# Row loads and stores of a DoRA forward kernel on one DMA ring in a fixed order

## The chip, the cores and the metric

The kernel runs on one core of one Trainium2 chip. The time is device microseconds (us) of one execution. A profile shows one execution under the hardware profiler; its span (163.3 us for the kernel before) is about 1.8 us shorter than the device time.

## The reference

```python
x: (16, 2048, 256) f32     W: (256, 256)     lora_A: (256, 16)     lora_B: (16, 256)     m: (256,)
W_adapted = W + scale * (lora_A @ lora_B)
W_final = W_adapted / sqrt(sum(W_adapted ** 2, axis=0) + 1e-8) * m
y = x.reshape(-1, 256) @ W_final           # (32768, 256) f32, as large as x
```

`W_final` is small. The work is to read 33.55 MB of `x`, multiply each row by a 256 x 256 matrix, and write 33.55 MB of `y`.

## The kernel before

The rows go through in 8 blocks of 4096 rows, 4.19 MB each. A block is loaded into one of five buffers by SyncE. TensorE transposes it in 8 chunks, VectorE copies a chunk to bf16, TensorE multiplies, and ScalarE copies the product back over the same place of the block's buffer. When the block is done, ScalarE issues its store. So there are two rings of DMA work: SyncE's with all loads and ScalarE's with all stores.

```python
xpool = ctx.enter_context(tc.tile_pool(name="xpool", bufs=5))
def load_x(b):
    t = xpool.tile([P, DJ, IN], FP32, name="x_sb", tag="x_sb")      # 128 x 32 x 256: 32 KB a partition
    nc.sync.dma_start(out=t, in_=x_flat[b * BLK : (b + 1) * BLK].rearrange("(p j) k -> p j k", p=P))
    return t
# ... loads of W, lora_A, lora_B, m; w_final is computed in about 17 us ...
for b in range(NBLK):                      # 8
    x_sb = load_x(b)
    for c in range(DJ // J):               # 8 chunks
        # ... 8 transposes into xt_ps, cast to xt_sb (VectorE), 8 matmuls into y_ps ...
        nc.scalar.copy(out=x_sb[:, c * J : (c + 1) * J, :], in_=y_ps)
        if c + 1 in store_after[b]:        # at the block's end; the last block in three parts
            nc.scalar.dma_start(out=..., in_=x_sb[:, j0:j_stored, :])
```

Below, L0 to L7 are the loads of the blocks and S0 to S7 their stores.

## Time and profile before

| what | value |
|---|---|
| time | 165.1 us, median of 3 runs (165.06 to 165.16) |
| span of the profile | 163.3 us |
| DMA rings | loads 48.9%, stores 48.0% of the 16 engines' span |
| rate while only loads run (5 to 35 us) | 428 to 432 GB/s |
| rate while both rings run (50 to 125 us) | 428 to 433 GB/s |
| rate while only stores run (130 to 155 us) | 429 to 432 GB/s |
| a 32 KB packet, median, on either ring | 1213 ns |
| first transposes, last copy of a result | 14 us, 151.3 us |

The rates are the bytes of the trace's DMA packets in stretches of 5 us, a packet's bytes spread over its time. Here are lines of the page of the kernel before: the span, the rows of 40 equal time slices (each digit is a busy share in tenths, 9 meaning 90% or more, and the last row is GB/s), the two rings with packets, megabytes and share of 16 engines' time, and the shares of the chain of work that ended last.

```profile
span 163.3 us, 2370 instructions
...
PE   0049888888888888888888888898889888886000
...
DMA  6999998999999899999999999999999999999992
GB/s 197 414 474 401 449 450 381 474 425 377 389 425 474 385 470 425 387 482 409 421 466 393 458 429 393 492 393 421 474 401 441 429 409 466 409 413 429 407 425 86
...
q1 hardware_dynamic: 1424, 33.82, 48.9%
q10 hardware_dynamic: 1746, 33.59, 48.0%
...
PE 57%; DVE 26%; DMA 4%; issue 2%; ACT 1%; DVEq 1%; ACTq 1%
```

The reader is to see two things that seem to contradict each other. The DMA row is at 9 (twice 8) from the second slice to the last but one: the 16 DMA engines never rest. Yet the chain that ended last is 57% TensorE and 26% VectorE, as if compute were the limit. The end of that chain, in order of time (start, length, what), settles it:

```profile
149.20 1.06 PE y_ps L158 x8
...
150.28 1.01 ACT x_sb L165
```

The last result is copied at 150.3 us and its store is issued at 151.3 us, but the span is 163.3 us long and the last store lands at 162.3 us. A store of 1 MB alone is an estimated 2.4 us of work at 431 GB/s; it took 11 us because other stores were ahead of it. So two things run side by side: a chain of compute of some 137 us, hidden, and a stream of transfers that starts at 2 us, never stops and ends at 162 us. The stream looks like the limit; e1 and e2 below test it. Its rate is 428 to 433 GB/s in the table above.

SyncE's own waits in the kernel before (in total, times, longest) show that the later loads wait for a buffer to be stored, which is harmless while the engines have other work:

```profile
SPq L52 <- DMA out_dram<-x_sb: 92.8, 3, 54.9
```

### The profile page before, as it was taken

What the parts mean: (1) busy time and instruction counts of PE and PEld (TensorE: products, weight loads), DVE (VectorE), ACT (ScalarE), POOL (GpSimd) and SP (SyncE); (2) the same over time, 40 slices, a digit from 0 to 9 for tenths busy, and PEclk for the clock granted to TensorE, in tenths of its full rate; (3) what the DMA queues carried; (4) which work ended last, traced back from release to release, by engine and by line L of the source; (5) the groups of instructions that cost most, each with busy time, mean ns of one, the idle gap of its engine ahead of it and who ended that gap; (6) DMA issues with size and microseconds to landing.
All of it is one profiled execution on the core that took longest, in us unless ns stands there. A gap on an engine that the chain in (4) does not pass through costs nothing.

```text
span 163.3 us, 2370 instructions
## 1 busy us (share of the span) xinstructions
PE 125.4 (77%) x1034; PEld 107.9 (66%) x1034; DVE 81.1 (50%) x76; ACT 66.1 (40%) x67; POOL 0.7 (0%) x6
## 2 busy tenths in 40 slices
PE   0049888888888888888888888898889888886000
PEld 0028677777777777777778777777887777774000
DVE  0145755555555555554555455545554555455000
ACT  3001244443544444444444364427441844085000
POOL 1000000000000000000000000000000000000000
PEclk9999999999999999999999999999999999999955
DMA  6999998999999899999999999999999999999992
GB/s 197 414 474 401 449 450 381 474 425 377 389 425 474 385 470 425 387 482 409 421 466 393 458 429 393 492 393 421 474 401 441 429 409 466 409 413 429 407 425 86
DMA packets 3180, 67.55 MB, mean 414 GB/s; under 512 B 593, under 2 KB 866, under 8 KB 866
## 3 DMA queue, kind: packets, MB, share of 16 engines
q1 hardware_dynamic: 1424, 33.82, 48.9%
q10 hardware_dynamic: 1746, 33.59, 48.0%
q8 instruction: 8, 0.13, 0.3%
q14 instruction: 2, 0.02, 0.0%
HBM read 33.85 MB, written 33.55 MB: 413 GB/s over the span
## 4 chain that ended last, share of the span: by engine, by line
PE 57%; DVE 26%; DMA 4%; issue 2%; ACT 1%; DVEq 1%; ACTq 1%
PE y_ps L158 33%; DVE xt_sb L153 23%; PE xt_ps L147 22%; DMA m_row<-in_m_dram 4%; PE n_ps L115 1%; DVE rnorm L124 1%; DVEq L206 1%; PE mb_ps L91 1%; ACT x_sb L165 1%; DVE w_final L126 0%; DVE sq L110 0%; DVE wa L106 0%; ACTq L60 0%; ACTq L64 0%; ACT norm L119 0%
## 5 line engine op out<-in xcount | busy, mean ns | idle before, releaser
L153 DVE CAST xt_sb<-xt_ps 128x1024 bf16<-128x1024 f32 x64 | 75.4, 1220 | 56.6 <-PE xt_ps L147 42.2
L165 ACT COPY x_sb<-y_ps 128x1024 f32<-128x1024 f32 x64 | 64.1, 1013 | 72.5 <-PE y_ps L158 72.4
L158 PE MATMUL y_ps<-w_final,xt_sb 128*128 128x256 bf16 x512 | 65.5, 273 | 11.5 <-DVE xt_sb L153 11.5
L147 PE MATMUL xt_ps<-identity,x_sb 128*128 128x128 f32 x512 | 68.7, 279 | 3.4 <-DVE xt_sb L153 3.1
L147 PEld LDWEIGHTS xt_ps<-identity,x_sb 128*128 128x128 f32 x512 | 58.7, 144 | 7.8 <-DVE xt_sb L153 6.7
L158 PEld LDWEIGHTS <-xt_sb 128*128 128x128 bf16 x512 | 47.8, 98 | 22.8 <-DVE xt_sb L153 18.2
L91 PE MATMUL mb_ps<-m_row,ones 1*128 1x256 f32 x2 | 1.2, 694 | 4.6 <-DMA m_row<-in_m_dram 4.6
L119 ACT ACTIVATE norm<-n_ps,eps_col 128x256 f32<-128x256 f32 x1 | 0.5, 473 | 10.4 <-PE n_ps L115 10.4
L91 PEld LDWEIGHTS mb_ps<-m_row,ones 1*128 1x128 f32 x2 | 0.5, 304 | 5.0 <-DVE aT L88 5.0
L82 DVE CAST b_bf<-b_nat 16x256 bf16<-16x256 f32 x1 | 0.3, 280 | 6.5 <-DMA b_nat<-in_lora_B_dram 6.5
L86 PE MATMUL aT_ps<-identity,a_nat 128*16 128x128 f32 x2 | 0.6, 394 | 3.8 <-DMA a_nat<-in_lora_A_dram 3.8
L115 PE MATMUL n_ps<-sq,ones 128*128 128x256 f32 x4 | 2.1, 674 | 1.5 <-DVE sq L110 1.5
L124 DVE RECIPROCAL rnorm<-norm 128x256 f32<-128x256 f32 x1 | 1.8, 1753 | 2.0 <-ACT norm L119 2.0
L86 PEld LDWEIGHTS aT_ps<-identity,a_nat 128*16 128x16 f32 x2 | 0.1, 88 | 3.8 <-issue 3.8
L115 PEld LDWEIGHTS n_ps<-sq,ones 128*128 128x128 f32 x4 | 1.2, 323 | 2.2 <-DVE sq L110 2.0
L76 ACT ACT_TABLE_LOAD x1 | 1.3, 1283 | 2.3 <-issue 2.3
L93 DVE COPY m_all<-mb_ps 128x256 f32<-128x256 f32 x1 | 0.4, 424 | 2.1 <-PE mb_ps L91 2.1
L126 DVE TENSOR_TENSOR w_final<-wam,rnorm 128x256 bf16<-128x256 f32 x2 | 0.8, 424 | 0.0
L122 DVE TENSOR_TENSOR wam<-wa,m_all 128x256 f32<-128x256 f32 x2 | 0.8, 418 | 0.0
L110 DVE TENSOR_TENSOR sq<-wa 128x512 f32<-128x512 f32 x1 | 0.7, 693 | 0.0
L106 DVE SCALAR_TENSOR_TENSOR wa<-ab_ps,w_nat 128x512 f32<-128x512 f32 x1 | 0.7, 692 | 0.0
L97 PE MATMUL ab_ps<-b_bf,aT 16*128 16x256 bf16 x2 | 0.6, 416 | 0.0
(11 smaller groups left out, 2.0 us busy)
## 6 DMA issues: line engine op xcount, KB each, us to landing
x_sb<-in_x_dram SPq DMA_DIRECT2D x8, 4096.0 KB, 31.2
out_dram<-x_sb ACTq DMA_DIRECT2D x7, 4096.0 KB, 27.9
out_dram<-x_sb ACTq DMA_DIRECT2D x1, 2048.0 KB, 12.4
out_dram<-x_sb ACTq DMA_DIRECT2D x2, 1024.0 KB, 11.0
w_nat<-in_W_dram SPq DMA_DIRECT2D x1, 256.0 KB, 2.8
a_nat<-in_lora_A_dram ACTq DMA_DIRECT2D x1, 16.0 KB, 2.9
b_nat<-in_lora_B_dram ACTq DMA_DIRECT2D x1, 16.0 KB, 6.2
m_row<-in_m_dram ACTq DMA_DIRECT2D x1, 1.0 KB
```

Of the source, the lines that this page charges most:

```text
L76: nc.scalar.activation(out=warm, in_=eps_col, func=AF.Sqrt)
L86: nc.tensor.transpose(aT_ps[:, c * P : (c + 1) * P], a_nat[:, c, :], identity)
L91: nc.tensor.matmul(mb_ps, ones[0:1, :], m_row, start=True, stop=True)
L115: nc.tensor.matmul(n2_ps, ones, sq[:, c, :], start=(c == 0), stop=(c == KC - 1))
L122: nc.vector.tensor_mul(out=wam[:, c], in0=wa[:, c], in1=m_all)
L124: nc.vector.reciprocal(out=rnorm, in_=norm)
L126: nc.vector.tensor_mul(out=w_final[:, c], in0=wam[:, c], in1=rnorm)
L147: nc.tensor.transpose(xt_ps[:, kc, j * P : (j + 1) * P], x_sb[:, c * J + j, kc * P : (kc + 1) * P], identity,)
L153: nc.vector.tensor_copy(out=xt_sb, in_=xt_ps)
L158: nc.tensor.matmul(y_ps[:, j, :], xt_sb[:, kc, j * P : (j + 1) * P], w_final[:, kc, :], start=(kc == 0 and (j % (J // 2)) == 0), stop=(kc ...
L165: nc.scalar.copy(out=x_sb[:, c * J : (c + 1) * J, :], in_=y_ps)
L206: with _tile.TileContext(nc) as tc:
```

## The change

The intent: all row transfers on SyncE's ring, in an order that the program fixes, with the first five loads issued at once and every later load behind a store whose buffer it needs.

```diff
+    ctx.enter_context(tc.manual_schedule(engines={mybir.EngineType.SP}))
 ...
+    x_tiles = {}
+    for b in range(XBUFS):                       # XBUFS = 5
+        x_tiles[b] = load_x(b)
     for b in range(NBLK):
-        x_sb = load_x(b)
+        x_sb = x_tiles[b]
 ...
-                nc.scalar.dma_start(
+                nc.sync.dma_start(
                     out=out_flat[...], in_=x_sb[:, j0:j_stored, :])
+        if b >= 1 and b - 1 + XBUFS < NBLK:
+            x_tiles[b - 1 + XBUFS] = load_x(b - 1 + XBUFS)
```

`manual_schedule` keeps the scheduler from reordering SyncE. Its instruction order becomes L0 L1 L2 L3 L4 S0 S1 L5 S2 L6 S3 L7 S4 S5 S6 and S7 in three parts. The change is thus two changes: the ring of the stores, and the order.

More of the change, by code (lines that the diff above doesn't have):

```diff
@@ L37 @@
     DJ = 32
+    XBUFS = 5
     BLK = DJ * P
@@ L44 @@
     startup = ctx.enter_context(tc.tile_pool(name="startup", bufs=1))
-    xpool = ctx.enter_context(tc.tile_pool(name="xpool", bufs=5))
+    xpool = ctx.enter_context(tc.tile_pool(name="xpool", bufs=XBUFS))
     xtpool = ctx.enter_context(tc.tile_pool(name="xtpool", bufs=2))
```

## The prediction

> **What bounds the kernel now.** The 16 DMA engines. The page's queue part gives ring q1 (SyncE: loads) 48.9% and ring q10 (ScalarE: stores) 48.0% of the engines' span, together 97%. Summing the trace's DMA packets in 5 us stretches gives about 431 GB/s whether only loads run (5 to 35 us: 428 to 432), both rings (50 to 125 us: 428 to 433, each about half) or only stores (130 to 155 us: 429 to 432). A 32 KB packet takes a median of 1213 ns on either ring. So the rate depends neither on direction nor on the number of rings. The engines are saturated from about 2 to 159 us.
>
> Compute is nearly as long but hidden: the chain of waits runs from 14 us (first transposes) to 151.3 us (last copy) on TensorE and VectorE without a DMA wait, 16.8 us a block; then 8 us of store backlog drains, and the last landing is at 162.3 us of a 163.3 us span.
>
> **What the change does.** The same 67 MB in the same transfers. Ten issues of 0.34 us leave ScalarE, which is busy 40% and not critical. SyncE's order becomes L0 to L4, S0, S1, L5, S2, L6, S3, L7, S4 to S6, then S7 in three parts. Loads and stores no longer share packet by packet, and a SyncE wait for a store also holds back the loads behind it.
>
> **Does the ring run dry?** One 4.19 MB transfer takes 9.7 us at 431 GB/s. Estimate from the trace's compute times (blocks end at 34.1, 50.9, 67.6, 84.4, 101.1, 117.9, 134.6, 151.3): L4 lands at about 53, S0 63, S1 72, L5 82, S2 92, L6 101, S3 111, L7 121, S4 131, S5 140, S6 150, S7 160. Every item is queued before the ring gets to it; the closest is S6, queued at 134.6 with work until 140. L5 is needed at about 98, L6 at 114, L7 at 131: 10 to 16 us of slack. So compute keeps its pace, the engines stay saturated and the end is bytes over rate, as before.
>
> [...]
>
> **Details.** When stores first start (36 to 39.5 us) the total dips to 300 to 400 GB/s: an estimated 0.7 us lost, once; load packets there take 1.8 us instead of 1.21. I expect one such dip still, near 53 us, as none recurs at later stores before. If instead every change from load to store costs one (four changes), the kernel gets 2 us slower; if it vanishes, 0.7 us faster. The spread of engines at the end (last landing 1.3 us after the one before) may move by tenths.
>
> **Prediction.** 165.0 us, 8 in 10 between 164.3 and 166.4. Faster by over 2%: 1%; within 2%: 93%; slower by over 2%: 6%.
>
> **What would show it.** Right: DMA row still 9s throughout, one ring with some 97%, compute from 14 to 151 us with no DMA wait, a tail of 8 to 11 us, landings near my list. Wrong: tenths below 9 in the DMA row mid-kernel, TensorE waiting for an x_sb load, compute ending later than 152 us.
>
> **What would make it wrong.** A loss at each load/store change on one ring; a limit on transfers queued on one ring; SyncE waking late after a landing; more uneven engines at the end.

The 165.0 us is bytes over the measured rate, as before the change, with no loss added for the ring. That a SyncE wait for a store also holds back the loads behind it was not shown by the profile before; x3 below shows it (L5 issued 10.4 us after its buffer was free, behind S3).

## The result, and the profile after

| | before | after |
|---|---|---|
| time | 165.13 us (165.06 to 165.21, 4 runs) | 165.47 us (165.40 to 165.85, 4 runs) |
| ratio | 1 | 1.0025 (95% interval 1.0008 to 1.0043) |
| span of the profile | 163.3 us | 163.6 us |
| last result copied, its store issued | 151.3 us | 149.9 us |
| last store: median engine landed, last engine landed | 160.81, 162.34 us | 160.89, 162.68 us |

A ratio is the mean time of one kernel's fast runs over that of the other's fast runs of the same rounds, so it is not quite the ratio of the medians. The change does nothing to speak of: a quarter of a per cent slower. The page after, the same lines as before:

```profile
span 163.6 us, 2378 instructions
...
PE   0049888888888888888888888888888888883000
...
DMA  6998998999999999999999999999999999999992
GB/s 196 421 481 385 425 473 380 481 409 392 485 409 368 401 477 401 435 457 388 449 441 409 461 409 433 441 411 437 441 425 433 429 425 449 409 429 413 423 403 92
...
q1 hardware_dynamic: 2864, 67.37, 96.7%
...
q10 hardware_dynamic: 306, 0.03, 0.1%
...
PE 55%; DVE 26%; DMA 4%; issue 4%; ACT 1%; DVEq 1%; ACTq 1%
```

The DMA row is still 9s (again two 8s), and one ring now has what two had: 96.7% against 48.9 + 48.0%. Only the small loads of `lora_A`, `lora_B` and `m` are left on the other ring. The end of the chain after:

```profile
147.77 1.06 PE y_ps L167 x8
...
148.86 1.01 ACT x_sb L174
```

Compute ends 1.4 us earlier (149.9 instead of 151.3 us), as the blocks are shorter (TensorE's instruction order came out different): 16.4 us a block up to block 4, then 16.7, where every block took 16.8 before. That gain lies wholly off the limiting stream and is lost in the backlog of stores: the tail from the last copy to the last landing grows from 11.0 to 12.8 us. SyncE's instructions in order of time after the change (start, length of the group, what; a group's length includes the waits between its issues):

```profile
1.23 2.86 SPq L53 DMA_DIRECT2D x_sb<-in_x_dram  x5
34.05 16.79 SPq L179 DMA_DIRECT2D out_dram<-x_sb  x2
65.52 0.34 SPq L53 DMA_DIRECT2D x_sb<-in_x_dram  x1
66.94 0.33 SPq L179 DMA_DIRECT2D out_dram<-x_sb  x1
75.21 0.34 SPq L53 DMA_DIRECT2D x_sb<-in_x_dram  x1
83.39 0.33 SPq L179 DMA_DIRECT2D out_dram<-x_sb  x1
94.62 0.34 SPq L53 DMA_DIRECT2D x_sb<-in_x_dram  x1
99.77 50.45 SPq L179 DMA_DIRECT2D out_dram<-x_sb  x6
```

The five loads are issued at once; S0 and S1 are issued when their blocks are done, 34.05 and 50.5 us; then loads and stores alternate as written. No compute instruction waits for a load in the middle of the kernel. The only wait of this kind in the list of waits is at the start:

```profile
PEld xt_ps L156 <- DMA x_sb<-in_x_dram: 0.6, 1, 0.6
```

The landings confirm the queue that the prediction worked out. The semaphore of each row transfer is raised 16 times in the trace, read here as once by each engine; the median of the 16 is given (us):

```
            L4    S0    S1    L5    S2    L6     S3     L7     S4     S5     S6     S7 (last part)
predicted   53    63    72    82    92    101    111    121    131    140    150    160
measured    53.0  62.8  72.6  82.2  92.0  101.6  111.6  121.3  131.4  141.0  151.2  160.9
```

### The profile page after: what moved, and what is told of

It reads as the page before. It is cut to its first block, busy times and chain, and to the rows that moved or that the text cites. A ratio compares the mean times of both kernels' runs of the same rounds, so it can differ in the third digit from the quotient of the medians.

```text
span 163.6 us, 2378 instructions
## 1 busy us (share of the span) xinstructions
PE 124.0 (76%) x1034; PEld 107.9 (66%) x1034; DVE 81.1 (50%) x76; ACT 66.8 (41%) x67; POOL 0.7 (0%) x6
## 3 DMA queue, kind: packets, MB, share of 16 engines
q1 hardware_dynamic: 2864, 67.37, 96.7%
## 4 chain that ended last, share of the span: by engine, by line
PE 55%; DVE 26%; DMA 4%; issue 4%; ACT 1%; DVEq 1%; ACTq 1%
PE y_ps L167 35%; DVE xt_sb L162 23%; PE xt_ps L156 17%; DMA m_row<-in_m_dram 4%; PE n_ps L118 1%; DVE rnorm L127 1%; DVEq L217 1%; PE mb_ps L94 1%; ACT x_sb L174 1%; DVE w_final L129 0%; DVE sq L113 0%; DVE wa L109 0%; ACTq L67 0%; ACTq L63 0%; ACT norm L122 0%
## 5 line engine op out<-in xcount | busy, mean ns | idle before, releaser
L174 ACT COPY x_sb<-y_ps 128x1024 f32<-128x1024 f32 x64 | 64.8, 1013 | 70.4 <-PE y_ps L167 69.8
L167 PE MATMUL y_ps<-w_final,xt_sb 128*128 128x256 bf16 x512 | 66.7, 273 | 14.9 <-DVE xt_sb L162 14.6
L156 PE MATMUL xt_ps<-identity,x_sb 128*128 128x128 f32 x512 | 67.4, 277 | 0.0
L167 PEld LDWEIGHTS <-xt_sb 128*128 128x128 bf16 x512 | 46.8, 98 | 28.1 <-DVE xt_sb L162 23.7
L156 PEld LDWEIGHTS xt_ps<-identity,x_sb 128*128 128x128 f32 x512 | 59.3, 144 | 1.3 <-DMA x_sb<-in_x_dram 0.6
## 6 DMA issues: line engine op xcount, KB each, us to landing
out_dram<-x_sb SPq DMA_DIRECT2D x2, 1024.0 KB, 12.8
```

What stands on the lines that cost most here:

```text
L156: nc.tensor.transpose(xt_ps[:, kc, j * P : (j + 1) * P], x_sb[:, c * J + j, kc * P : (kc + 1) * P], identity,)
L167: nc.tensor.matmul(y_ps[:, j, :], xt_sb[:, kc, j * P : (j + 1) * P], w_final[:, kc, :], start=(kc == 0 and (j % (J // 2)) == 0), stop=(kc ...
```

## The experiments

Theory A: the 16 DMA engines bound both kernels. Number of rings and order are neutral as long as something is always queued; the change's only danger is that its ring runs dry. Rival B: the TensorE and VectorE chain bounds both kernels, as the chain of waits seems to say, and the change left it alone. Rival C: the single ring costs something and the order gives it back.

All runs were made beside runs of the kernel before on the same chip. The twelve runs, with the kernel before at 165.16 to 165.25 us:

| run | time, median | ratio to before (95% interval) |
|---|---|---|
| e1 half the compute | 165.46 us | 1.0013 (0.9995 to 1.0031) |
| e2 half the load bytes | 156.11 us | 0.9439 (0.9424 to 0.9453) |
| e3 fixed order, two rings | 165.21 us | 0.9994 (0.9980 to 1.0008) |
| e4 one ring, scheduler's order | 189.98 us | 1.1483 (1.1465 to 1.1502) |
| x4 one ring, four loads ahead | 166.07 us | 1.0045 (1.0023 to 1.0066) |
| x3 one ring, three loads ahead | 191.08 us | 1.1552 (1.1508 to 1.1597) |
| x3 two rings, three buffers | 185.63 us | 1.1212 (1.1157 to 1.1267) |
| d1 staggered | 168.61 us | 1.0212 (1.0179 to 1.0245) |
| d2 flat | 169.59 us | 1.0267 (1.0250 to 1.0284) |
| d3 staggered, rows apart | 168.69 us | 1.0211 (1.0189 to 1.0233) |
| d4 flat, rows apart | 169.73 us | 1.0283 (1.0252 to 1.0314) |
| w stagger by W | 168.53 us | 1.0206 (1.0189 to 1.0224) |

### e1: take half of the compute away

```diff
-                for kc in range(KC):              # transposes, KC = 2
+                for kc in range(1):
-            nc.vector.tensor_copy(out=xt_sb, in_=xt_ps)
+            nc.vector.tensor_copy(out=xt_sb[:, 0], in_=xt_ps[:, 0])
-            for kc in range(KC):                  # matmuls
+            for kc in range(1):
```

> The changed kernel with half of the TensorE and VectorE work taken away (only one of the two 128-wide halves of the input dimension is transposed, cast and multiplied; the result is wrong on purpose). All 67 MB still move. Theory A (the 16 DMA engines bound both kernels, compute hides behind them): the time stays at 165.4 us within 0.7 us, compute of a block falls from 16.7 to some 9 us and now waits for x_sb loads; the DMA row stays at 9s. Rival B (the TensorE and VectorE chain bounds both kernels, and the change left it alone): the time falls by about half of the 134 us chain, to under 115 us.

The time is 165.46 us, the same. Rows of its page, and a line of its list of waits (in total, times, longest):

```profile
PE   0148698888889687000029840498206870000000
...
PEclk9999999999999999955555996559965997555555
DMA  5998989989999999999999999999999999999980
```

```profile
PE xt_ps L156 <- DMA x_sb<-in_x_dram: 37.6, 4, 20.2
```

The chain that ended last, as shares of the span, is another one here:

```profile
DMA 62%; PE 11%; DVE 5%; ACT 2%; ACTq 1%; issue 1%; SPq 0%
```

TensorE is now empty for whole slices, waiting 37.6 us for loads, and even its granted clock falls to 5 tenths there; the DMA row has not changed and neither has the time. Rival B, which asked for under 115 us, has fallen. A chain of waits made mostly of TensorE does not say that TensorE is the limit: the chain is followed back from the last instruction of the program's end, and that was compute whose output still had 11 us of queue in front of it.

### e2: take half of the load bytes away

```diff
-            out=t, in_=x_flat[...].rearrange("(p j) k -> p j k", p=P),
+            out=t[:, : DJ // 2, :], in_=x_flat[...].rearrange(...)[:, : DJ // 2, :],
-                        x_sb[:, c * J + j, kc * P : (kc + 1) * P],
+                        x_sb[:, (c % (CH // 2)) * J + j, kc * P : (kc + 1) * P],
```

> The changed kernel loading only half of each block (the second half of the compute reuses the first half's place; wrong result on purpose), so 50.6 MB move instead of 67.4, about 117 us at 431 GB/s. Theory A: the DMA engines no longer bind; compute keeps its 16.7 us a block and ends at about 150 us, the store backlog behind it is gone (tail about 5 us instead of 12), so 157 us (155 to 159). Rival B (chain of compute plus a fixed tail): the time stays at 165.

The time is 156.11 us, inside theory A's 155 to 159. The rows of its page and the end of its chain:

```profile
PE   0398788888889988888888888888999888888400
...
DMA  5999999169903996699899999999039930998991
```

```profile
144.84 1.06 PE y_ps L167 x8
...
145.93 1.01 ACT x_sb L174
```

Now the DMA row has holes, and compute is the limit for most of the span: the last copy ends at 146.9 us and the last store lands at 153.3 us, 6.3 us behind its issue instead of 12.8 us in the changed kernel. Together e1 and e2 give both limits: transfers 165 us, compute about 156 us as it runs in e2 (its first block is done at 31.8 us instead of 34.05 us, so part of the gain is an earlier start). What binds is the transfers; the runs do not separate the 16 engines from what lies behind them. While the transfers bind and the ring does not run dry, order and rings have little to change: 0.9994 and 1.0025 of the time before in e3 and the changed kernel.

### e3 and e4: each half of the change alone

e3 keeps the fixed order and lookahead and gives the stores back to ScalarE's ring:

```diff
-                nc.sync.dma_start(
+                nc.scalar.dma_start(
                     out=out_flat[...], in_=x_sb[:, j0:j_stored, :])
```

> The changed kernel with its fixed load order and lookahead of five, but the ten stores back on ScalarE's ring: undoes the single ring alone. Theory A (ring count is neutral while the engines always have queued work): between the two kernels, 165.0 to 165.5 us; the one dip of the rate (about 0.7 us of engine time) moves back to about 36 us, where the first store starts. Rival C (the single ring itself loses a little at each change of direction, and the order gains it back): 164.6 us or less.

It took 165.21 us, the same as the kernel before (0.9994). e4 is the opposite: the kernel before with only the stores moved to SyncE, and the scheduler free to order them:

```diff
-                nc.scalar.dma_start(
+                nc.sync.dma_start(
                     out=out_flat[...], in_=x_sb[:, j0:j_stored, :])
```

> The kernel before with only the ten stores moved to SyncE: one ring, but the scheduler's own order. The instruction order shows SyncE as L0 L1 L2 S0 S1 L3 S2 L4 S3 L5 S4 L6 S5 L7 S6 S7: L3 stands behind the wait of S1 for the end of block 1. Theory A with the queue model of the prediction: the ring runs dry from about 33 to 35 us and 45 to 51 us, L3 lands at about 71 instead of 43 us, block 3 waits about 5 us and later blocks about 3 us each, 177 us (172 to 181). A rival for which SyncE's order does not matter, as the five buffers are free anyway: 165 us.

It took 190 us in its three fast runs (189.58 to 190.07; the fourth, profiled, was slow at 195.14). The four kernels make a table of two by two (ratios to the kernel before):

| | scheduler's order | fixed order, five loads ahead |
|---|---|---|
| two rings | 1 | 0.9994 |
| one ring | 1.148 | 1.0025 |

So rival C is half right, at another scale than it said: the two halves of the change do offset each other, but what the single ring costs in the scheduler's order is not a loss at each change of direction. It is 15%, and the fixed order removes it. On two rings the order changes nothing, and it had little to change: the kernel before has its first five loads issued by 4.1 us as well. e4's instruction order on SyncE is L0 L1 L2 S0 S1 L3 S2 L4 S3 L5 S4 L6 S5 L7 S6 S7: the buffers for L3 and L4 are free from the start, but the instructions stand behind the waits of S0 and S1 for the end of a block. S0 and S1, then L3, in its profile (of the slow execution, but with the same order of instructions):

```profile
36.95 16.80 SPq L170 DMA_DIRECT2D out_dram<-x_sb  x2
...
53.80 0.42 SPq L52 DMA_DIRECT2D x_sb<-in_x_dram  x1
```

Theory A named the place and the sign; its size (177 us, 172 to 181) was a miss by 13 us. What shows of the reason is read below from x3, which has the same SyncE order.

### x3 and x4: how far ahead the loads must stand

The changed kernel with fewer buffers and therefore fewer loads ahead, and the kernel before with three buffers:

```diff
-    XBUFS = 5
+    XBUFS = 4            # x4_one_ring;  3 in x3_one_ring;  bufs=3 in x3_two_rings
```

> The changed kernel with four buffers and four loads ahead instead of five, SyncE order L0 to L3, S0, S1, L4, S2, L5, S3, L6, S4, L7. Queue model: the ring always has work (closest: S1 queued at 51 with work until 53 us) and L7 lands about 3 us before its block, so as the changed kernel within 0.7 us: 165.5 us (164.9 to 167). If the model is too kind by some us, L7 is late and the time goes over 167.

> The changed kernel with three buffers and three loads ahead: SyncE's order is then L0 L1 L2 S0 S1 L3 S2 L4 ..., exactly that of the run with one ring and the scheduler's own order, which had five buffers and took 190 us. Theory A (it is the order on the ring, not the buffers): 190 us (187 to 192). Rival (the scheduler's order with five buffers was slow for another reason): another time, some 177 us as the queue model without the falling clock had it, or more than 195 as buffers are now short as well.

> The kernel before with three x buffers instead of five: two rings, but a load must wait for the store of its buffer. Queue model, now with the TensorE clock that falls to half in a wait[...], as the run of one ring without the fixed order showed: blocks wait for loads from block 4 on, 182 us (174 to 186), shorter than the 190 us of one ring in the order with three loads ahead, since here a waiting store does not hold back the load behind it. Rival (order on a ring does not matter, only the buffers): the same as the 190 us.

Four loads ahead are nearly enough: 166.07 us, as expected in time. The margin was not: L7 was to land 3 us before its block, and TensorE waited 1.9 us for it, at 134.5 us. Three are not enough. With three, SyncE's order is exactly e4's, and the time is nearly e4's: 191.08 against 189.98 us, though e4 has five buffers. In e4 the number of buffers can't be the cause, so it is the order on the ring. Three buffers on two rings take 185.63 us, so in x3 most of the loss would be there without the single ring; the two losses do not add up. The profile of x3 with one ring (a fast run), first rows of its page, then SyncE's instructions in order of time, then a line of its list of waits:

```profile
PE   1168999998999800999789950698969980199960
...
PEclk9999999999999985599999995589999997569996
DMA  7999998792299999999479999999857999982695
```

```profile
33.78 16.80 SPq L179 DMA_DIRECT2D out_dram<-x_sb  x2
50.68 0.37 SPq L53 DMA_DIRECT2D x_sb<-in_x_dram  x1
...
94.33 0.33 SPq L179 DMA_DIRECT2D out_dram<-x_sb  x1
94.75 0.38 SPq L53 DMA_DIRECT2D x_sb<-in_x_dram  x1
```

```profile
PE xt_ps L156 <- DMA x_sb<-in_x_dram: 27.4, 5, 9.2
```

L3, which in the changed kernel is issued at 2.7 us and lands at 42.8 us, is issued here at 50.7 us, right behind S1, which had to wait for the end of block 1. Its buffer was not free before S0 had landed on all engines, at 47.0 us; the last 3.6 us are due to the order alone, and in e4, where the buffer was free from the start, so is all of the wait until 53.8 us (in its list of SyncE's waits, loads wait 0.2 us in all and stores 180 us). The ring had nothing to do from 45 us, when S0 landed (the two 2s in the DMA row). L3 lands from 72.6 to 74.6 us and block 3 waits for it since 66.6 us. Then S3 is issued only at 94.3 us, so L5 behind it at 94.8 us, though its buffer was free at 84.4 us, when S2 had landed. The same happens again two blocks later. So in this trace the wait of one transfer is a wait of SyncE, and what stands behind it in SyncE's order is not issued: L5 was held back 10.4 us behind S3. That is what the second ring buys here: not bandwidth (428 to 433 GB/s with two rings before the change, 425 to 433 with one after it), but a second issuing engine that can stand in a wait.

What lengthens this run beyond the 177 us of the queue model, which had no falling clock, shows in part in three stretches of the same profile (length, then busy us and instruction count of each engine, then the granted TensorE clock as a share, DMA share, GB/s):

```profile
core 0: us, PE busy (x) PEld busy (x) DVE busy (x) ACT busy (x) POOL busy (x), PEclk, DMA share, GB/s
66.00:75.00 9.00, 0.26 (x2) 0.29 (x3) 0.00 (x0) 0.58 (x1) 0.00 (x0) 0.67 1.01 376
75.00:81.00 6.00, 6.00 (x37) 5.50 (x37) 2.45 (x2) 1.01 (x1) 0.00 (x0) 0.64 1.00 431
81.00:94.00 13.00, 10.84 (x93) 9.12 (x91) 7.07 (x6) 6.78 (x7) 0.00 (x0) 1.00 0.82 352
```

While TensorE waits, its granted clock falls, and it stays low for the first part of the next block: 0.64 on average from 75 to 81 us. The profile's clock records have it at half in three waits, from 2.3 to 3.6 us after the last matmul before the wait until 4.4 to 4.6 us after the first matmul behind it. The block took 19.7 us from the last landing of L3 to the issue of S3 instead of 16.4. Not all of these 3.3 us are the clock's: 4.6 us at half clock lose an estimated 2.3 us (in e4's profile 16 transposes took 3.65 us where the clock was 0.50, and 1.94 us where it was 1.00), and block 4, which ran at full clock but whose load came too late for its start to overlap the end of block 3 (TensorE waited 1.0 us), took 17.9 us. Besides, packets took longer than their usual 1213 ns, most of it where the ring changes between stores and loads: 6.5 us in all for each engine in this run, against 1.95 us in the changed kernel. How the missing 13 us divide between clock, overlap and packets is not shown. The expectation for two rings with three buffers had the clock in it: 182 us, measured 185.63 (fast runs; its fourth run, the profiled one, was slow). There loads and stores are issued by two engines, and the kernel is 3% faster than one ring with the same lookahead (185.63 against 191.08 us).

### d1 to d4: what is the dip at the first change of direction?

In every profile of a kernel with full rings the rate falls once, at the first meeting of loads and stores. "Excess" below is the time that packets took above the median of their size (1213 ns for 32 KB, 611 for 16, 309 for 8, 46 for 1), summed and divided by 16 engines. By ten-microsecond stretches it is 0.71 us from 30 to 40 us in the kernel before and 0.62 us from 50 to 60 us in the changed one; the dip moves with S0, as predicted, and in e3 it is back at 30 to 40 us. It does not come back at the other changes of direction there (at most 0.13 us in a stretch). But x4, whose ring never ran dry, has a second one of 0.5 us two changes later, and e2, e4 and x3 with one ring have further ones of 0.7 to 1.3 us, each at the first one or two changes after the ring had been empty; and their very first store, issued to an empty ring, has none. Theory S was that a change is dear only where all engines make it in step. Four small extra loads behind L0 were to put the engines out of step (13, 10, 7, 4 partitions of 8 KB) or, as a control, to leave them in step (16 each). The 1.2 us in the expectations is the author's estimate, four packets of 8 KB at 309 ns, and supposes one partition for each engine; how the packets fell to the engines is not shown, but 15 of the 16 landings of L3 lay within 1.9 us in d1, against 0.5 us in the changed kernel:

```diff
     x_tiles[0] = load_x(0)
+    last = xpool.tile(...)                       # the fifth block's buffer, loaded properly later
+    for i, p in enumerate((13, 10, 7, 4)):       # d2: (16, 16, 16, 16)
+        nc.sync.dma_start(out=last[0:p, i * 8 : (i + 1) * 8, :],
+                          in_=x_flat[0 : p * 8].rearrange("(p j) k -> p j k", p=p))
     # then the loads of blocks 1 to 4; d3 and d4: the same with rows 32 KB apart
```

> The changed kernel with four extra loads behind the first block's, of 13, 10, 7 and 4 partitions of 8 KB (0.28 MB, into a tile that a later load fills), so that the DMA engines run out of step by up to 1.2 us in steps of 0.31. Question: what is the dip of the rate at the first change from load to store (a mean of 0.6 to 0.9 us of engine time above the 1213 ns per packet)? Theory S (the change is dear only where all engines make it in step): the packets' excess around 45 to 60 us falls from 0.75 us per engine to 0.25 or less; time 165 to 166.3 us, as the most loaded engines carry 1.2 us more. Rival F (the first store, or a first change of a ring, costs once): the excess stays at 0.6 to 0.9 us.

> Control of the staggered run: the same four extra loads, but each of 16 partitions, so that every engine carries the same 1.2 us more and they stay in step. Both theories: the dip stays, 0.6 to 0.9 us of excess per engine around 45 to 60 us; time 166.2 to 167.2 us.

> As the staggered run before it, which cost 3.4 us instead of 0.2 to 1 us because its four extra loads, all from one stretch of 128 KB, ran slowly (4 us at 110 to 200 GB/s). Here the extra loads (13, 10, 7, 4 partitions of 8 KB) read rows 32 KB apart, which the fifth block's load reads again. Theory S (the first change of direction is dear where the engines make it in step): excess around the first change under 0.25 us per engine, time 165 to 166.3 us. Rival G (step has nothing to do with it, since the flat control lost its dip too with the landings still within 0.4 us): the same excess here and in the flat run of the same call.

> Control: four extra loads of 16 partitions each from rows 32 KB apart, 1.2 us more for each engine, engines in step. Theory S: the dip is there, 0.6 to 0.9 us of excess per engine around the first change, time 166.3 to 167.2 us. Rival G: the excess is the same as in the staggered run.

The times failed everywhere: 168.6 to 169.7 us, more than 2 us above the ranges expected. The dip was gone in all four runs (0.03 to 0.08 us of excess around the first change), as theory S had it for d1 and d3, but in the controls too, where 14 of the 16 landings of the load before the change still lay within 0.5 us (0.6 us in the changed kernel, which has the dip). So theory S falls, and so does "the first store costs once"; rival G of d3 and d4, for which step does not matter, stands. What the runs leave standing is only the place: the dear changes are among the first ones after the ring started or had run empty, and none was dear after the extra loads had disturbed the engines early. The cause stays open. It is worth 0.7 us in both kernels, so it does not decide between them.

Where the extra time is lost can be read off. It is lost early: the excess from 10 to 20 us is 3.0 to 3.8 us in the four runs, which lost 3.1 to 4.3 us. It is not that the extra rows of d1 came from one stretch of 128 KB, as the expectation of d3 said: rows 32 KB apart took the same time (168.69 against 168.61 us). A stretch of d2 while the extra loads run (columns as above):

```profile
14.50:16.00 1.50, 1.50 (x8) 1.50 (x9) 1.44 (x1) 0.03 (x1) 0.00 (x0) 1.00 1.06 120
```

The rate is 120 GB/s (104 GB/s in the same stretch of d4), about a quarter of 431, though the 16 engines are busy (DMA share 1.06, and 0.99 in d4). Why is not shown: the extra loads all went to partitions 0 to 15, and no run chose others.

### w: an attempt at a faster version

If the dip could be removed for nothing, 0.6 us could be won. W is loaded anyway; loaded in uneven pieces it was to put the engines out of step without one byte more:

```diff
+    x_tiles = {0: load_x(0)}
-    nc.sync.dma_start(out=w_nat, in_=W.rearrange("(c p) o -> p c o", p=P))
+    for p in (27, 39, 22, 25, 15):
+        nc.sync.dma_start(out=w_nat[p0 : p0 + p], in_=W.rearrange(...)[p0 : p0 + p]);  p0 += p
```

> A try at a faster version: the changed kernel, with the first block's load put ahead of W, and W loaded in five pieces of 27, 39, 22, 25 and 15 partitions[...]. Compute starts some 4 us later, hidden. Theory S: the first dip (0.6 us) goes, the engines end closer, 164.9 us (164.5 to 165.2), a hair below both kernels. Rival G: 165.4 to 166.2 us, no gain[...].

The run took 168.53 us, 2% slower, and is a miss for a reason of its own. A line of SyncE's waits:

```profile
SPq L68 <- DMA a_nat<-in_lora_A_dram: 11.1, 1, 11.1
```

The fifth piece of W (L68 is the line of its load) had to wait 11.1 us for the load of `lora_A`, which has nothing to do with W. In the traces of the kernel before and the changed one, the landings of all 22 transfers raise only eight semaphores, each used by two or three transfers; that the piece was to use the same one as `lora_A` is the author's reading and was not tested. L1 behind it was issued at 14.2 us, and from 13.5 to 15.5 us the ring was all but empty (35 GB/s on average against 432), an estimated 1.8 us of the 3.1 us lost against the changed kernel. As in e4, a wait on SyncE kept the loads behind it from being issued. The dip was there (1.08 us of excess from 50 to 60 us), but the run says little on step: 15 of the 16 landings of L3 lay within 0.7 us, against 0.5 in the changed kernel and 1.9 in d1. No version beats the kernel before.

## Why the prediction was right

- "The 16 DMA engines" as the limit: right in that the transfers bind and compute does not, shown by e1 (half the compute, 165.46 us) and e2 (half the load bytes, 156.11 us). That it is the engines themselves, and not what lies behind them, was not tested; in d2 they are as busy (DMA share 1.06) at about a quarter of the rate (120 GB/s).
- "The rate depends neither on direction nor on the number of rings": right, 425 to 433 GB/s on one ring in every stretch of 5 us from 10 to 155 us after the change, the dip's apart, and e3 within 0.1% of the kernel before.
- "Does the ring run dry?" No: the measured landings are within 1.2 us of the list. This was the step on which all hung, and e4 and x3 show that it was no formality. With the loads standing two places further back, the same argument gives a slow kernel (177 us expected), and the chip confirms it, slower still, at 1.15.
- One dip near 53 us instead of 36 us: right in place (49.5 to 54 us) and size (0.62 us from 50 to 60 us, and the four changes did not cost one each: 0.04 to 0.10 us around the later three from load to store). "If every change costs one" was a risk that it named; e2, e4 and x3 show that it was real, since after an empty ring some changes do cost 0.7 to 1.3 us. Why the changed kernel is spared is not known (d1 to d4), so this part was right from the pattern of the trace and not from a cause.
- Compute "from 14 to 151 us": it ended at 149.9 us. The shorter blocks were not foreseen. They were off the critical path, so they cost the forecast nothing; but the tail, forecast at 8 to 11 us, is 12.8 us to the last landing (11.0 us to the median one).
- The time: 165.0 us forecast, 165.47 measured, inside 164.3 to 166.4. The forecast sum had no term for the 0.34 us. In the two profiles the median engine ends at the same time (160.81 and 160.89 us) and the last one 0.34 us later. The mean excess is 0.29 us larger (1.95 against 1.66). In the three one-ring profiles with a full ring (changed kernel, e1, x4) single packets at the first change took up to 1.6 to 2.0 us more than the median, and the last engine landed 1.8 to 3.3 us after the median one; in the two with two rings (before, e3) it was 0.8 to 1.3 us and 1.5 us. So one ring seems to leave the engines less even. That is one profile of each kernel, and no run isolates it. The times point the same way: with the same order on two rings (e3) the ratio is 0.9994, on one ring 1.0025, and the two intervals just touch.

Where the expected gain of such a change goes: there was none to have. The order could pay only where engines idle for want of queued transfers, and before the change they did not idle.

## What to carry to other kernels

First ask what the transfers add up to: bytes over the measured rate, whether the DMA row has holes, and whether the GB/s row keeps to the measured rate (in d2 a slice at 9 moved only 172 GB/s). Where there were none and it did, as here, rings and order were worth nothing (0.9994 to 1.0025 of the time before), though the chain of waits was 83% compute; take half the compute away once to be sure (165.46 us here). The second issuing engine was not bandwidth here (428 to 433 GB/s with it, 425 to 433 without) but a second place to wait: if loads and stores are put on one ring, write the order down, and check that each transfer is queued before the one ahead of it ends, because one store that waits for compute holds back every load behind it (15% here).
